# A chain of two transformer blocks on one core: the feed-forward network in seven block products, its weights' sums on VectorE, the modulation beside the dilated attention, block-diagonal states

## The chip, the core and the metric

The kernel runs on one core of a Trainium2 chip. The core has a matrix engine (TensorE, PE in the rows; its weight loads are listed apart as PEld), a vector engine (VectorE, DVE), a scalar engine (ScalarE, ACT), a general engine (GpSimd, POOL) and SyncE (SP), which here only issues DMAs. The metric is the device time of one execution in microseconds (us). Matrix results land in eight banks of PSUM of 128 x 512 fp32; everything else works in SBUF, 128 partitions wide.

## The reference

x has 512 tokens of 1024 features. The first block has two layers (i = 0 with a pooling mixer, i = 1 with dilated attention); the second has two layers with three branches. Cut to what matters here:

```python
def _swiglu(x, w_gate, w_up, w_down):          # 1024 -> 2816 -> 1024
    return (jax.nn.silu(x @ w_gate) * (x @ w_up)) @ w_down

def first_block(x, ...):
    for i in range(DEPTH):                     # DEPTH = 2
        h = _swiglu(x, ffn1_w_gate[i], ffn1_w_up[i], ffn1_w_down[i])
        x = _layer_norm(ALPHA * x + MACARON_WEIGHT * h, ln_gain[i, 0], ln_bias[i, 0])
        m = _pool_mixer(...) if i % N_MIXERS == 0 else _dilated_attention_mixer(...)
        x = _layer_norm(ALPHA * x + m, ln_gain[i, 1], ln_bias[i, 1])
        h = _swiglu(x, ffn2_w_gate[i], ffn2_w_up[i], ffn2_w_down[i])
        x = _layer_norm(ALPHA * x + MACARON_WEIGHT * h, ln_gain[i, 2], ln_bias[i, 2])

def second_block(x, c, ...):
    c_act = jax.nn.silu(c)
    for l in range(DEPTH):
        mod = c_act @ ada_w[l] + ada_b[l]      # the modulation: one row of 3 x 1024
        shift, scale, gate = jnp.split(mod, 3, axis=-1)
        h = rms_norm(x, pre_norm[l]) * (1.0 + scale[:, None]) + shift[:, None]
        p = split_proj(h @ w_in[l])
        # retention and gla: 4 heads, keys of 64, values of 128; per chunk
        #   o = scores @ v + q @ state;  state = decay * state + k.T @ v
        # dsa_attention: sparse attention over the top 128 keys; then the merge
        x = x + gate[:, None] * rms_norm(y, post_norm[l])
```

## The kernel before

**Arithmetic.** Large products are made from split operands: a = h + l, h the rounded copy in the matrix engine's fast fp32 format and l the rest. `mm3` makes three matmuls of them, h·h, h·l and l·h (in the trace L146 to L148). The class `Stream` feeds weights: it loads chunks of up to 1 MB through SP's queue into two raw buffers (`wraw`), cuts them into parts of 128 x 1024 and splits each: ScalarE makes `wh` (L75), VectorE `wl` = raw - wh (L76), every fifth part GpSimd. It runs four parts ahead of the products (`split_ahead`), with five buffers each.

**Stages.** In the profile: first network of layer 0 from 10 to 384 us, pooling mixer to 489, second network to 858; layer 1: first network to 1246, dilated attention to 1860, second network to 2217; then the second block's layers to 2788 and 3362.

**The network (`ffn`).** Its 2816 hidden columns are 22 tiles of 128, in two halves of 12 and 10. A pair of tiles, called a unit in what follows, takes four parts of weights (two of gate, two of up) and 4 x 24 matmuls of 512 columns (eight contraction rows, three each). ScalarE makes silu (L366) and the split's h (L373); VectorE the product (L370) and the split's l (L374). The first four parts are done in two halves of the tokens (`f1_first`, 192 matmuls of 256 columns), since the last tokens' input comes late: it goes through transpositions on PE (L259), ScalarE (`xTh`, L267) and VectorE (`xTl`, L268). After a half, `f2` makes the down product of its rows, 512 columns of the output at a time, and VectorE adds it to x (L384, L386). In the last down product the last 8 rows of weights are kept back and done token tile by token tile (`tail=8`), and the layer norm of a tile (`layer_norm_tile`, L275 to L292) follows as soon as it has its sum; the next stage's transpositions follow that.

**Modulation.** `ada` makes shift, scale and gate with VectorE (L923, 192 operations on weights that GpSimd's queue loads, L920), sums over partitions with a product of ones on PE (L940, L941) and sends the rows to memory. A background generator (`early`, rate 0.09) is advanced by the foreground's ticks and spreads this over the first four stages.

**States.** In `retention` and `gla` the four heads of a token tile are done in two halves (p), each on 64 partitions of the queries: per half two matmuls of 128 columns with the scores and, from the second tile on, two with the state (L1171 and L1173; L1363 and L1365), into one bank per half.

**Order.** Each engine works through its own instructions in order. The Tile framework's scheduler decides that order when the kernel is built, from the order of the code and the dependences; PSUM banks and SBUF buffers are handed on when their last reader is done. In the dilated attention the scores of a group go PE (L675), VectorE (bias, L690, and row maximum, L693), ScalarE (exponential, L694), PE (transposition, L701), ScalarE (L703), PE (values, L713 and L717).

## Time and profile before

| | |
|---|---|
| median of 3 runs | 3365.49 us (3364.72 to 3367.86) |
| profiled execution | 3364.3 us |
| its span, first to last instruction | 3362.2 us |
| granted TensorE clock, mean | 0.999 |
| busy: PE, PEld, DVE, ACT, POOL | 99%, 80%, 49%, 34%, 15% |
| DMA, mean | 98 GB/s |

Busy time of overlapping matmuls is counted once. A row's duration of a matmul of 512 columns is some 0.4 us, more than the distance to the next one's start, since matmuls are pipelined: what one costs is read from starts. fp32 products that aren't split show two records per matmul. All rows of a helper have one line, so a tile's name tells where it belongs.

### The profile page before, as it was taken

The numbers are of one execution on the slowest core, as the hardware profiler recorded it, in microseconds if no ns is written. First come the engines' busy times: TensorE is split into PE (matmuls) and PEld (weight loads), VectorE is DVE, ScalarE is ACT, GpSimd is POOL, SyncE is SP. The second block draws the span as 40 slices with busy tenths as digits, with TensorE's granted clock in tenths as the row PEclk, the third lists the DMA queues.
The fourth block names the chain that finished last, engine by engine and source line by source line (L and its number), as shares of the span: only waits on it lengthen the run. The fifth ranks groups of instructions, "written<-read, shape, count | busy, mean of one in ns | idle before, by whom it ended". The sixth has DMA issues, their size and how long they took to land.

```text
span 3362.2 us, 44608 instructions
## 1 busy us (share of the span) xinstructions
PE 3326.0 (99%) x18469; PEld 2685.8 (80%) x18469; DVE 1663.9 (49%) x2936; ACT 1151.5 (34%) x1769; POOL 502.7 (15%) x558
## 2 busy tenths in 40 slices
PE   9999999999999999999999999999999999999998
PEld 7888888888888888788787888878778788777877
DVE  4444773334643353433435432366864736594563
ACT  3222233222222224444444322233434533343442
POOL 2211211212211121111110100021111001111000
PEclk9999999999999999999999999999999999999999
DMA  5433423333433223222222323232122332222222
GB/s 169 137 116 125 146 95 108 117 121 129 132 122 110 94 69 107 64 71 69 82 70 76 119 88 100 94 104 89 57 82 75 108 100 92 69 82 76 76 88 75
DMA packets 278771, 328.29 MB, mean 98 GB/s; under 512 B 10197, under 2 KB 222393, under 8 KB 278569
## 3 DMA queue, kind: packets, MB, share of 16 engines
q1 hardware_dynamic: 268504, 294.36, 26.5%
q0 software_dynamic: 9920, 31.03, 2.9%
q8 instruction: 145, 2.38, 0.3%
q14 instruction: 58, 0.47, 0.0%
q10 hardware_dynamic: 144, 0.07, 0.0%
HBM read 319.10 MB, written 6.32 MB: 97 GB/s over the span
## 4 chain that ended last, share of the span: by engine, by line
PE 90%; DVE 6%; DMA 1%; issue 1%; POOL 1%; ACT 1%; POOLq 0%; DVEq 0%; ACTq 0%
PE bank L146 27%; PE bank L148 27%; PE bank L147 27%; PE bank L701 1%; DVE wl L76 1%; PE bank L675 1%; DVE work L1115 1%; DVE m L1114 1%; PE bank L713 1%; PE bank L1077 1%; PE bank L717 1%; DMA adaw<-in_ada_w_dram 1%; PE bank L1417 1%; PE bank L1399 1%; PE bank L259 0%
## 5 line engine op out<-in xcount | busy, mean ns | idle before, releaser
L75 ACT ACTIVATE wh<-wraw 128x1024 fp32r<-128x1024 f32 (+1 forms) x528 | 554.1, 1052 | 1351.9 <-PE bank L147 616.1
L146 PE MATMUL bank<-xTh,wh 128*128 128x512 f32 (+1 forms) x2624 | 1009.5, 385 | 3.0 <-ACT wh L75 1.8
L147 PE MATMUL bank<-xTl,wh 128*128 128x512 f32 (+1 forms) x2624 | 996.6, 380 | 2.5 <-DVE xTl L268 2.5
L148 PE MATMUL bank<-xTh,wl 128*128 128x512 f32 (+1 forms) x2624 | 996.7, 380 | 0.7 <-DVE wl L76 0.7
L76 DVE TENSOR_TENSOR wl<-wraw,wh 128x1024 fp32r<-128x1024 f32 (+1 forms) x422 | 521.7, 1237 | 730.2 <-ACT wh L75 724.8
L146 PEld LDWEIGHTS bank<-xTh,wh 128*128 128x128 f32 x2624 | 494.7, 189 | 118.8 <-issue 15.6
L148 PEld LDWEIGHTS bank<-xTh,wl 128*128 128x128 f32 x2624 | 495.5, 189 | 103.7 <-DVE wl L76 1.2
L147 PEld LDWEIGHTS bank<-xTl,wh 128*128 128x128 f32 x2624 | 496.1, 189 | 98.4 <-DVE xTl L268 3.0
L76 POOL TENSOR_TENSOR wl<-wraw,wh 128x1024 fp32r<-128x1024 f32 (+1 forms) x106 | 255.6, 2411 | 1595.2 <-ACT wh L75 1525.8
L146 PE MATMUL bank<-wh,xTh 128*128 128x512 f32 (+2 forms) x1024 | 372.1, 364 | 1.4 <-ACT xTh L267 1.4
L148 PE MATMUL bank<-wh,xTl 128*128 128x512 f32 (+2 forms) x1024 | 363.9, 356 | 0.6 <-DVE xTl L268 0.6
L147 PE MATMUL bank<-wl,xTh 128*128 128x512 f32 (+2 forms) x1024 | 363.6, 355 | 0.0
L146 PE MATMUL bank<-wh,ah 128*128 128x512 f32 x704 | 278.3, 395 | 0.0
L148 PE MATMUL bank<-wh,al 128*128 128x512 f32 x704 | 278.0, 395 | 0.0
L147 PE MATMUL bank<-wl,ah 128*128 128x512 f32 x704 | 278.0, 395 | 0.0
L146 PEld LDWEIGHTS bank<-wh,xTh 128*128 128x128 f32 x1024 | 192.5, 188 | 33.6 <-ACT xTh L267 2.4
L148 PEld LDWEIGHTS bank<-wh,xTl 128*128 128x128 f32 x1024 | 192.6, 188 | 30.0 <-DVE xTl L268 1.1
L147 PEld LDWEIGHTS bank<-wl,xTh 128*128 128x128 f32 x1024 | 193.0, 188 | 26.1 <-issue 0.4
L923 DVE SCALAR_TENSOR_TENSOR modn<-adaw,cols,modn 128x256 f32<-128x256 f32 x192 | 101.4, 532 | 185.7 <-DMA adaw<-in_ada_w_dram 182.1
L370 DVE SCALAR_TENSOR_TENSOR v<-g,bank 128x512 f32<-128x512 f32 x88 | 60.5, 688 | 259.2 <-PE bank L148 255.7
L148 PEld LDWEIGHTS bank<-wh,al 128*128 128x128 f32 x704 | 132.2, 188 | 31.9
L146 PEld LDWEIGHTS bank<-wh,ah 128*128 128x128 f32 x704 | 132.3, 188 | 31.6
(354 smaller groups left out, 3256.9 us busy)
## 6 DMA issues: line engine op xcount, KB each, us to landing
wraw<-in_w_in_dram SPq DMA_DIRECT2D x58, 1024.0 KB, 4.8
wraw<-in_ffn_w_gate_dram SPq DMA_DIRECT2D x43, 1024.0 KB, 4.9
wraw<-in_ffn_w_up_dram SPq DMA_DIRECT2D x43, 1024.0 KB, 4.9
wraw<-in_ffn_w_down_dram SPq DMA_DIRECT2D x40, 1024.0 KB, 5.0
wraw<-in_attn_w_qkv_dram SPq DMA_DIRECT2D x56, 512.0 KB, 3.6
adaw<-in_ada_w_dram POOLq DMA_DIRECT2D x96, 256.0 KB, 3.4
wraw<-in_attn_w_qkv_dram SPq DMA_DIRECT2D x8, 1024.0 KB, 5.4
wraw<-in_w_out_dram SPq DMA_DIRECT2D x8, 1024.0 KB, 5.0
```

The source lines that it names most:

```text
L75: nc.scalar.activation(h, raw, AF.Copy)
L76: (nc.gpsimd if self.nsplit % POOL_EVERY == 1 else nc.vector).tensor_tensor(lo, raw, f32(h), ALU.subtract)
L146: nc.tensor.matmul(ps, s[0], m[0], start=start, stop=False)
L147: nc.tensor.matmul(ps, s[0], m[1], start=False, stop=False)
L148: nc.tensor.matmul(ps, s[1], m[0], start=False, stop=stop)
L370: nc.vector.scalar_tensor_tensor(v, gs[j - 2], 0.5, ps, op0=ALU.mult, op1=ALU.mult)
L675: nc.tensor.matmul(ps[g - 1][r * 32:(r + 1) * 32, 256:], q[g][:, r * P + i * 32:r * P + (i + 1) * 32], kk[g][:, :, r * P:(r + 1) * P], sta ...
L701: nc.tensor.transpose(ps[:, j * P:(j + 1) * P], p[:, j * P:(j + 1) * P], k.ident)
L713: nc.tensor.matmul(ps[c:c + 64, :E], t[:, j * P + c:j * P + c + 64], v0[:, i + j, hh, :], start=j == 0, stop=False, tile_position=(0, c))
L717: nc.tensor.matmul(ps[r * 32:(r + 1) * 32, :E], t[:, (g + 1) * P + r * 32:(g + 1) * P + (r + 1) * 32], vr[g - 1][r][:, h, :], start=False, ...
L923: nc.vector.scalar_tensor_tensor(m, w[:, i, :], k.cols["c_2"][:, kt:kt + 1], m, op0=ALU.mult, op1=ALU.add)
L1077: k.nc.tensor.matmul(ps[:, :n], q, ks[i][:, g, :n], start=i == 0, stop=i == 1)
```

## The change

1. **Gate and up as seven products.** The hidden columns are 11 units of 256, in four groups (`FF_PARTS`). The first unit of a network is done as before. For each other one, tokens (two halves), contraction (two halves) and columns (gate, up) make 2 x 2 blocks, and seven products of blocks take the place of eight: 7 x 24 matmuls of 256 columns. Four sums of weight blocks per unit are made on VectorE, in place in the raw buffers but one (`wsum`), from a second pair of raw buffers (`wraw2`) for up; the sums of input blocks (`token_sums`) once per network. All parts of units are split by ScalarE and VectorE, none by GpSimd. Products share banks: what one bank holds after one product is read out (copy by ScalarE, L528ff.) and the next product is added on.
2. **The down product** comes in four groups, and `tail` is 4.
3. **Modulation** is a background generator at rate 0.38 beside the dilated attention, drained after it, with rows of 256 columns.
4. **States** are kept block-diagonal, 128 x 256 for a pair of heads with zeros (GpSimd) where keys and values belong to different heads; `gather_heads` makes four matmuls of 128 columns and two of 256 on all 128 partitions into one bank.

```diff
+class Units:
...
+    def order(self):
+        res = []
+        for u in range(len(self.units)):
+            res.append((u, "b11"))
+            if u:
+                res.append((u - 1, "t4"))
+            res.append((u, "b21"))
+            if u:
+                res.append((u - 1, "b22"))
+            res += [(u, n) for n in ("t2", "t1", "t3")]
+        return res + [(len(self.units) - 1, n) for n in ("b22", "t4")]
...
+    def block(self, own, what):
...
+        if what == "t2":
+            t3 = K.wsum.tile([P, n * b11.shape[2]], F32, name="wsum", tag="wsum").rearrange("p (a b) -> p a b", a=n)
+            self.sums[own] = t3
+            add(t3, b22, b12, ALU.subtract)
+            add(b11, t3, b11, ALU.add)
+        elif what == "t1":
+            add(b12, b22, b11, ALU.subtract)
+        elif what == "t4":
+            add(b21, b21, b11, ALU.subtract)
...
-            (nc.gpsimd if self.nsplit % POOL_EVERY == 1 else nc.vector).tensor_tensor(lo, raw, f32(h), ALU.subtract)
+            pool = self.nsplit % POOL_EVERY == 1 and not isinstance(what, str)
+            (nc.gpsimd if pool else nc.vector).tensor_tensor(lo, raw, f32(h), ALU.subtract)
...
-FF_HALVES = ((0, 12), (12, 22))
+FF_PARTS = ((0, 3), (3, 6), (6, 9), (9, 11))
+HS = S // 2
...
+def token_sums(k, pool, tmp):
...
+    for n in ("a11", "a21", "a22"):
+        whole(n)
+    a11, a21, a22 = [full[n] for n in ("a11", "a21", "a22")]
+    V.tensor_tensor(a22, a21, a22, ALU.add)
+    V.tensor_tensor(a21, a11, a21, ALU.subtract)
+    new("s1")
+    nc.scalar.activation(res["s1"][0], a22, AF.Copy)
+    V.tensor_tensor(a11, a22, a11, ALU.subtract)
+    V.tensor_tensor(res["s1"][1], a22, f32(res["s1"][0]), ALU.subtract)
...
-def ffn(k, st, a, name, i, lnj, post, tail=8):
+def ffn(k, st, a, name, i, lnj, post, tail=4):
...
+        def product(bank, name, first=False, last=False):
+            h, lo = st.next()
+            ah, al = A[name]
+            for j in range(2):
+                cs = slice(j * P, (j + 1) * P)
+                o = bank[:, j * HS:(j + 1) * HS]
+                for kt in range(4):
+                    for n, (x, y) in enumerate(((h, ah), (h, al), (lo, ah))):
+                        nc.tensor.matmul(o, x[:, kt, cs], y[:, kt, :], start=first and j == kt == n == 0,
+                                         stop=last and kt == 3 and n == 2, skip_group_check=True)
+                    k.tick(0.5)
+        def unit(u, before):
...
+            product(b, "a11", first=True)
+            p1 = tp2("ta")
+            nc.scalar.activation(p1, b, AF.Copy)
+            before(0)
+            ba = k.bank()
+            product(ba, "a12", first=True, last=True)
+            V.tensor_tensor(p1, p1, ba, ALU.add)
+            nc.scalar.activation(p1, p1, AF.Silu)
+            before(1)
+            product(b, "s2")
...
+            product(bc, "s1", first=True)
+            product(b, "s3")
...
+            V.tensor_tensor(c22, u3, bc, ALU.add)
+        def rest(u, s, step):
...
+                product(b, "a22", last=True)
...
+                V.scalar_tensor_tensor(c22, g2, 0.5, c22, op0=ALU.mult, op1=ALU.mult)
...
+                product(bc, "s4", last=True)
+                V.tensor_tensor(u2, u2, bc, ALU.add)
+                V.scalar_tensor_tensor(u2, g1, 0.5, u2, op0=ALU.mult, op1=ALU.mult)
...
+def gather_heads(k, at, v, q, state):
+    b = k.bank()
+    for h in range(RH):
+        k.nc.tensor.matmul(b[:, h * P:(h + 1) * P], at(h), v[:, h * P:(h + 1) * P], start=h == 0,
+                           stop=state is None and h == RH - 1, skip_group_check=True)
+    if state is not None:
         for hp in range(2):
+            k.nc.tensor.matmul(b[:, 2 * hp * P:(2 * hp + 2) * P], q(hp), state[:, hp, :, :].rearrange("p s e -> p (s e)"),
+                               start=False, stop=hp == 1, skip_group_check=True)
...
             if dilated:
                 k.drain()
+                k.bg(modulation(), 0.38, slow=True)
                 dilated_mixer(k, st, a, 1)
+                k.drain(slow=True)
```

**A unit on VectorE.** In the last network, before, VectorE's order has the low parts of weights (`wl`) between the gated products (`v`) and their splits (`al`):

```order
L370 SCALAR_TENSOR_TENSOR v_15289<-g_15225,bank_15260 128x512
L76 TENSOR_TENSOR wl_15334<-wraw_15228,wh_15333 128x1024
L374 TENSOR_TENSOR al_15292<-v_15289,ah_15291 128x512
L370 SCALAR_TENSOR_TENSOR v_15326<-g_15258,bank_15295 128x512
L76 TENSOR_TENSOR wl_15367<-wraw_15296,wh_15366 128x1024
L374 TENSOR_TENSOR al_15329<-v_15326,ah_15328 128x512
L76 TENSOR_TENSOR wl_15435<-wraw_15364,wh_15434 128x1024
L370 SCALAR_TENSOR_TENSOR v_15425<-g_15361,bank_15396 128x512
L76 TENSOR_TENSOR wl_15470<-wraw_15364,wh_15469 128x1024
L374 TENSOR_TENSOR al_15428<-v_15425,ah_15427 128x512
```

Now a unit there reads so; `wsum` and the `wraw` written are sums of weight blocks, `ta`, `tb` and `tc` results read out of banks:

```order
L145 TENSOR_TENSOR wl_19257<-wraw_19088,wh_19256 128x1024
L563 TENSOR_TENSOR tb_19056<-tb_19056,bank_19058 128x512
L145 TENSOR_TENSOR wl_19289<-wraw_18870,wh_19288 128x1024
L564 SCALAR_TENSOR_TENSOR tb_19056<-ta_18995,tb_19056 128x512
L120 TENSOR_TENSOR wraw_19088<-wsum_19382,wraw_19088 128x1024
L145 TENSOR_TENSOR wl_19319<-wraw_19088,wh_19318 128x1024
L494 TENSOR_TENSOR al_19153<-tb_19056,ah_19152 128x2x256
L122 TENSOR_TENSOR wraw_19154<-wraw_19154,wraw_19088 128x1024
L145 TENSOR_TENSOR wl_19351<-wraw_18872,wh_19350 128x1024
L124 TENSOR_TENSOR wraw_19088<-wraw_19088 128x1024
L145 TENSOR_TENSOR wl_19386<-wraw_19088,wh_19385 128x1024
L546 TENSOR_TENSOR tc_19346<-tc_19346,bank_19286 128x512
```

Three of the four sums of the next unit (L120, L122, L124) stand in VectorE's order among the low parts and gated products of the unit before; the fourth, L119, three rows ahead of these.

**The start of a network on VectorE.** In the second network, before, the last token tile's norm (`x3_80`) and the transposed input's low parts (`xTl`) were followed by two rows of the modulation and the weights:

```order
L268 TENSOR_TENSOR xTl_94<-bank_3845,xTh_93 128x4x128
L292 SCALAR_TENSOR_TENSOR x3_80<-x3_80,rstd_3734,B_2792 128x1024
L268 TENSOR_TENSOR xTl_94<-bank_3852,xTh_93 128x4x128
L268 TENSOR_TENSOR xTl_94<-bank_3859,xTh_93 128x4x128
L268 TENSOR_TENSOR xTl_94<-bank_3866,xTh_93 128x4x128
L943 COPY modn0_531<-bank_3888 128x512
L930 TENSOR_TENSOR adal_3926<-modn1_532,adah_3925 128x512
L76 TENSOR_TENSOR wl_4027<-wraw_3763,wh_4026 128x1024
L370 SCALAR_TENSOR_TENSOR v_4007<-g_4003,bank_3771 128x512
L76 TENSOR_TENSOR wl_4031<-wraw_3763,wh_4030 128x1024
```

Now sums of the input (`a11` to `a22`, `s1l`) and of weights stand there:

```order
L440 TENSOR_TENSOR a11_4741<-xTh_93,xTl_94 128x1024
L347 TENSOR_TENSOR xTl_94<-bank_4607,xTh_93 128x4x128
L347 TENSOR_TENSOR xTl_94<-bank_4614,xTh_93 128x4x128
L440 TENSOR_TENSOR a21_4743<-xTh_93,xTl_94 128x1024
L440 TENSOR_TENSOR a22_4745<-xTh_93,xTl_94 128x1024
L119 TENSOR_TENSOR wsum_4784<-wraw_4499 128x1024
L453 TENSOR_TENSOR a22_4745<-a21_4743,a22_4745 128x1024
L120 TENSOR_TENSOR wraw_4497<-wsum_4784,wraw_4497 128x1024
L454 TENSOR_TENSOR a21_4743<-a11_4741,a21_4743 128x1024
L458 TENSOR_TENSOR s1l_4750<-a22_4745,s1h_4749 128x1024
L457 TENSOR_TENSOR a11_4741<-a22_4745,a11_4741 128x1024
L145 TENSOR_TENSOR wl_4781<-wraw_4497,wh_4780 128x1024
```

Nine further rows follow (four of 512 columns and five of 1024) up to the low part of the first unit's t2 (`wl_4788`).

**The dilated attention on VectorE.** Before, bias (`sc`) and row maximum (`m`) of the scores stood with rows of the attention alone:

```order
L690 SCALAR_TENSOR_TENSOR sc<-dist,bank 128x256
L690 SCALAR_TENSOR_TENSOR sc<-dist,bank 128x128 x2
L690 SCALAR_TENSOR_TENSOR sc<-dist,bank 128x256
L693 TENSOR_REDUCE m<-sc 128x1
L690 SCALAR_TENSOR_TENSOR sc<-dist,bank 128x128 x2
L693 TENSOR_REDUCE m<-sc 128x1
L595 TENSOR_TENSOR q_12926<-bank,q_12926 64x4x4x32
```

Now the modulation's rows (`adam`, on the loaded `adaw`) stand among them:

```order
L896 SCALAR_TENSOR_TENSOR sc<-dist,bank 128x128 x2
L896 SCALAR_TENSOR_TENSOR sc<-dist,bank 128x256
L899 TENSOR_REDUCE m<-sc 128x1
L896 SCALAR_TENSOR_TENSOR sc<-dist,bank 128x128 x2
L1132 SCALAR_TENSOR_TENSOR adam<-adaw,cols,adam 128x256
L899 TENSOR_REDUCE m<-sc 128x1
L1132 SCALAR_TENSOR_TENSOR adam<-adaw,cols,adam 128x256 x2
L928 RECIPROCAL rc<-bank 128x1
L1132 SCALAR_TENSOR_TENSOR adam<-adaw,cols,adam 128x256
L931 TENSOR_SCALAR on<-bank,rc 128x64
L1132 SCALAR_TENSOR_TENSOR adam<-adaw,cols,adam 128x256
L145 TENSOR_TENSOR wl<-wraw,wh 128x1024
```

A row of `adam` whose weights are not there yet holds the rows below it.

## Rows read from the trace of the kernel before

**Rows 1.** The page: busy us (share of span) x instructions; the ending chain.

```profile
PE 3326.0 (99%) x18469; PEld 2685.8 (80%) x18469; DVE 1663.9 (49%) x2936; ACT 1151.5 (34%) x1769; POOL 502.7 (15%) x558
...
PE 90%; DVE 6%; DMA 1%; issue 1%; POOL 1%; ACT 1%; POOLq 0%; DVEq 0%; ACTq 0%
```

**Rows 2.** PE's waits: line, releaser: us in all, times, longest us.

```profile
PE bank L1283 <- DVE gz L1265: 7.1, 3, 3.9
...
PE bank L147 <- DVE xTl L268: 2.5, 2, 1.3
PE bank L259 <- DVE z L964: 2.1, 1, 2.1
```

**Rows 3.** Groups by line and shape: count | busy us, mean ns | idle before.

```profile
L75 ACT ACTIVATE wh<-wraw 128x1024 fp32r<-128x1024 f32 x516 | 545.6, 1059 | 1345.0 <-PE bank L147 615.2 <-PE bank L148 366.5 <-issue 281.2
L76 DVE TENSOR_TENSOR wl<-wraw,wh 128x1024 fp32r<-128x1024 f32 x413 | 514.3, 1246 | 725.3 <-ACT wh L75 720.0 <-PE bank L940 3.6
...
L76 POOL TENSOR_TENSOR wl<-wraw,wh 128x1024 fp32r<-128x1024 f32 x103 | 250.2, 2430 | 1557.6 <-ACT wh L75 1488.1 <-PE bank L1046 28.1 <-issue 26.1
...
L366 ACT ACTIVATE g<-bank 128x512 f32<-128x512 f32 x88 | 51.0, 579 | 0.0
```

**Rows 4.** PE's timeline from 539.60, first and last of 152: start, duration.

```profile
539.60 0.40 PE L148 MATMUL bank<-xTh,wl 128*128 128x512 f32 x1
...
574.97 0.40 PE L147 MATMUL bank<-xTl,wh 128*128 128x512 f32 x1
```

**Rows 5.** PE's timeline of 256 columns, 68 rows; engines' busy time within.

```profile
497.70 0.28 PE L148 MATMUL bank<-xTh,wl 128*128 128x256 f32 x1
...
505.56 0.28 PE L148 MATMUL bank<-xTh,wl 128*128 128x256 f32 x1
...
498.00:505.00 7.00, 7.00 (x62) 7.00 (x62) 6.74 (x10) 1.34 (x2) 1.45 (x1) 1.00 0.67 212
```

**Rows 6.** PE's timeline in retention, a half tile's products and four alike.

```profile
2336.55 0.60 PE L1171 MATMUL bank<-rv,rat 128*128 128x128 f32 x4
...
2346.70 0.38 PE L1171 MATMUL bank<-rv,rat 128*128 128x128 f32 x2
2347.01 0.49 PE L1173 MATMUL bank<-kv,rqk 64*128 64x128 f32 x2
...
2347.84 0.49 PE L1173 MATMUL bank<-kv,rqk 64*128 64x128 f32 x2
2348.26 0.51 PE L146 MATMUL bank<-xTh,wh 128*128 128x512 f32 x1
```

**Rows 7.** DVE's timeline in a network: start us, duration us.

```profile
334.19 1.22 DVE L76 TENSOR_TENSOR wl<-wraw,wh 128x1024 fp32r<-128x1024 f32 x1
335.32 0.48 DVE L923 SCALAR_TENSOR_TENSOR modn<-adaw,cols,modn 128x256 f32<-128x256 f32 x1
335.72 0.68 DVE L374 TENSOR_TENSOR al<-v,ah 128x512 fp32r<-128x512 f32 x1
```

**Rows 8.** DVE's and PE's timelines, second network, last transposed input.

```profile
506.94 1.29 DVE L268 TENSOR_TENSOR xTl<-bank,xTh 128x512 fp32r<-128x512 f32 x2 [2.11 <-ACT xTh L267]
...
506.47 0.36 PE L146 MATMUL bank<-xTh,wh 128*128 128x256 f32 x1
```

**Rows 9.** DVE's timeline at a network's end, one token tile to the next.

```profile
377.05 0.67 DVE L386 TENSOR_TENSOR x<-x,bank 128x512 f32<-128x512 f32 x1
...
381.85 0.69 DVE L386 TENSOR_TENSOR x<-x,bank 128x512 f32<-128x512 f32 x1
```

**Rows 10.** Dilated attention: PE PEld DVE ACT POOL busy; DVE's wait for modulation weights.

```profile
1246.00:1860.00 614.00, 612.09 (x4968) 488.53 (x4967) 265.66 (x554) 268.87 (x399) 94.09 (x134) 1.00 0.25 76
...
DVE modn L923 <- DMA adaw<-in_ada_w_dram: 182.1, 66, 5.7
```

**Rows 11.** ACT's and PE's timelines in dilated attention: exponential, then transposition.

```profile
1615.54 0.68 ACT L694 ACTIVATE sc<-sc,m 128x512 f32<-128x512 f32 x1
...
1617.35 0.33 PE L701 MATMUL bank<-ident,sc 128*128 128x128 f32 x1
```

More of the change, by code (lines that the diff above doesn't have):

```diff
@@ L30, with __init__ @@
 POOL_EVERY = 5
+class Units:
+    def __init__(self, units):
+        self.units = units
+    def order(self):
[9 more added lines that the diff above has]
+        return res + [(len(self.units) - 1, n) for n in ("b22", "t4")]
 class Stream:
-    def __init__(self, K, chunks, ahead):
+    def __init__(self, K, plan, ahead):
         self.K = K
-        self.chunks = chunks
-        self.parts = [(ci, p) for ci, (_, ps) in enumerate(chunks) for p in ps]
+        self.chunks = []
+        self.parts = []
+        for c in plan:
+            n = len(self.chunks)
+            if isinstance(c, Units):
+                for first, second in c.units:
+                    self.chunks += [(first, 0), (second, 1)]
+                for u, what in c.order():
+                    own = (n + 2 * u, n + 2 * u + 1)
+                    self.parts.append((own, what, {"t4": own[:1], "b22": own[1:]}.get(what, ())))
+                continue
+            src, ps = c
+            self.chunks.append((src, 0))
+            self.parts += [((n,), p, (n,) if i == len(ps) - 1 else ()) for i, p in enumerate(ps)]
+        self.place = []
+        count = [0, 0]
+        for _, q in self.chunks:
+            self.place.append(count[q])
+            count[q] += 1
+        self.gone = [set(), set()]
+        self.left = [0, 0]
         self.raw = {}
+        self.sums = {}
         self.ready = {}
@@ L61, in load @@
             self.nload += 1
+    def block(self, own, what):
+        K = self.K
+        first, second = [self.raw.get(c) for c in own]
+        n = (second if first is None else first).shape[1] // 2
+        b11, b21 = (None, None) if first is None else (first[:, :n], first[:, n:])
+        b12, b22 = (None, None) if second is None else (second[:, :n], second[:, n:])
+        add = K.nc.vector.tensor_tensor
+        if what == "t2":
[7 more added lines that the diff above has]
+            add(b21, b21, b11, ALU.subtract)
+        return {"b11": b11, "b21": b21, "b22": b22, "t1": b12, "t2": b11, "t4": b21, "t3": self.sums.get(own)}[what]
     def split(self, upto):
@@ L388, in evac @@
                         k.pend.append(layer_norm_tile(k, tp, t, G, B, post))
-                f2(k, st, acts.get, list(range(f0, f1)), 512, evac, tail=tail if fin else 0)
+                act = lambda kt: [x[:, kt % 2, :] for x in acts[kt // 2]]
+                f2(k, st, act, list(range(2 * u0, 2 * u1)), 512, evac, tail=tail if fin and c == 1 else 0)
         k.recent = None
@@ L1161, in scores @@
[L1161 to L1173 removed]
+            for p in range(2):
+                rows = slice(p * 64, p * 64 + 64)
+                nc.tensor.matmul(ps[p][:, hp * P:(hp + 1) * P], qk[rows, 2 + hp, ts], qk[rows, hp, ts], start=True, stop=True)
```

350 lines of the change are left out of this document (203 added, 147 removed).

## The prediction

> **What bounds the kernel now.** I read the page's busy times first and its chain of waits second. TensorE (PE) is busy 99% of the span and the chain runs through it for 90%; VectorE (DVE) is busy 49% [rows 1]. Third comes the list of what PE waits for: its largest entries are 7.1, 2.5 and 2.1 us [rows 2]. So PE's issue rate is the whole time, and a change counts only by the time that PE needs and by the waits it creates on PE. As rows of matmuls overlap, I take their cost from start to start. In the first feed-forward network after the pool mixer 152 matmuls of 512 columns start from 539.60 to 574.97: 35.37/151 = 0.2342 us each [rows 4]. There 68 of 256 columns start from 497.70 to 505.56: 7.86/67 = 0.1173 us each [rows 5]. Half the columns cost half the time, although weights are loaded without a pause there (PEld busy 7.00 of 7.00 us, same rows).
>
> By the Trainium skill's page TensorE: Matmul & The Clock Gate, section "Back-to-back issue gap", the spacing in a stream of load and matmul is set by both operations, and N/2.4 + 2.5 ns under-counts small matmuls (81 ns for 56 at N = 128); with those 25 ns on top of its 109 at N = 256, my estimate is 134 ns, and the change would save nothing in its units. The trace disagrees at 256 columns, with 117 ns against 234.
>
> The profiled execution took 3364.3 us, 2.1 more than its span; the median is 3365.5. I sum against 3364.3 and add 1.2 at the end.
>
> **The change part by part.**
>
> *Block products.* Each of the four networks has eleven units; ten become seven products of 24 matmuls of 256 columns. A unit was 96 x 0.2342 = 22.48 us and becomes 168 x 0.1173 = 19.71. 40 x 2.78 = 111 us less, if PE never waits.
>
> *VectorE in a unit.* Now eleven operations of 1024 columns (seven low parts, four sums) and seven of 512, where it had three or four low parts and four of 512. An operation of 1024 takes 1.22 us alone and 1.13 when another follows; of 512, 0.68 and 0.60 (starts 334.19, 335.32, 335.72) [rows 7]. So 16.6 to 18.4 us of PE's 19.7: 84 to 93%. GpSimd (POOL) no longer takes a part in five, which cost it 2430 ns [rows 3]. The splits run up to four parts, 11 us, ahead of PE, and with this lead VectorE has 1.3 us per unit to spare. I take 0 in the steady state; if the lead is lost, see case D. Where a group of units ends (16 places), the last two products stand alone: the last waits for ScalarE's copy (0.58, row of L366 [rows 3]) and an addition (0.69), 1.8 us with the hand-overs, under eleven matmuls of the product before and the four to seven of the down product that the order puts between, 2.2 to 2.9 us. From 0 to 0.5 each; 4 us, at most 8.
>
> *Start of a network.* The block products need sums of the transposed input. After the last low part of it, which begins at 506.94 and ends at 508.2 [rows 8], 14 operations of 1024 (1.2 us with hand-overs) and four of 512 (0.65) stand in VectorE's order up to the low part of t2: 19.4 us, to 527.6. PE has 120 matmuls of unit 0 left from 506.47 (14.1 us, to 520.5) and two products (5.6 us), and wants it at 526.1. It waits 1.5 us, and as much again for t1, 4.3 us later on VectorE and 2.8 on PE: 3 us. Four networks: +13 (0 to 25, as nothing else there gets longer).
>
> *End of a network.* The last down product was done token by token over 8 rows of weights, 24 matmuls or 5.62 us per tile, and now over 4: 2.81. VectorE's work on a tile, addition and layer norm, takes 4.80 us (377.05 to the same row at 381.85) [rows 9]. Before, it hid; PE waited 2.1 us at the worst end [rows 2]. Now PE passes from the tail to the next stage with 48 x 0.2342 = 11.2 us, 72 matmuls of 256 (8.4) and three transpositions of 0.8 (505.68, after the last row of [rows 5], to 506.47 [rows 8]): 22.0 us. VectorE ends the fourth tile at 2.8 + 4 x 4.80 = 22.0, plus some 5 us of transposed low parts (four of 512) and weight parts (two of 1024) between: 27.3. 5 us each, 6 at the last, whose transformation adds two operations: +21.5 (10 to 30).
>
> *Block-diagonal states.* A token tile with a state took two halves, and one half (two matmuls of 128 columns and two on 64 rows, each two records) goes from 2346.70 to 2348.26 and lets the next matmul start 0.1 late: 1.66 us [rows 6], 3.3 per tile. Now four matmuls of 128 columns are eight records of (0.60 - 0.38)/2 = 0.11 us (four records at 2336.55 and two at 2346.70 in the same rows), 0.88, and two of 256 columns four records of twice that, 0.88: with 0.1, 1.86. That is 1.46 less for 12 tiles (three tiles, retention and gated attention, two layers): -18. At the least nothing, if the one bank is waited for; I take the rows. The scores' new order is worth 0 to -5; I take -2. GpSimd's zero halves lie beside PE.
>
> *Down product and loads.* It comes in four parts instead of two, so 16 more additions of 512 columns per network (0.68 [rows 7]) beside its matmuls, where VectorE has only low parts to make: 0. The weights loaded are the same bytes.
>
> *Modulation.* PE does the same products. In the networks the old place cost nothing that a row shows. Beside the dilated attention VectorE is busy 265.66 of 614 us [rows 10], so there is room for 176 operations of 0.48 us (row at 335.32 [rows 7]; 16 of the 192 go early), 84 us. But VectorE works in order, and its queue there holds the attention's scores. Before, it waited 66 times for these weights, 182.1 us, 2.76 each [rows 10]; with two of four loads not ahead, 44 such waits remain. Behind each stand reduction, exponential and PE's transposition. The tight chain has little room: the exponential at 1615.54 lasts 0.68, and PE transposes it at 1617.35 [rows 11], 1.1 us later. A wait of 2.76 in it would cost 1.7; a sixth of the 44 in it is 12 us. The ends are 0 (all beside the chain) and 44 x 2.76 = 121 (all on it); the 614 us have many rows that are not in the chain, so I stay near 0: +12.
>
> **Sum.** -111 - 18 - 2 + 4 + 13 + 21.5 + 12 = -80.5; 3364.3 - 80.5 + 1.2 = 3285 us.
>
> **The rivals.**
>
> B: the stalls hide. VectorE's start and end queues may run back to back at 1.13 and 0.60, and the modulation fall between chains: 3285 less 0.75 x 50 = 3248. For it: before, no wait for a layer norm's output or a transposed low part is above 2.5 us [rows 2]. Against: 27.3 against 22.0 us is no close call.
>
> C: the dilated stage pays three times as much (36 instead of 12) and units lose 0.25 us each (10): 3285 + 34 = 3319. For it: 2.76 us per wait against a room of 1.1.
>
> D, slower than before: VectorE becomes the bound in the units. It is in order, and each of the four sums needs ScalarE's copy (L75, 1.06 us [rows 3]) before its low part can follow; if nothing lies between, that is 18.4 + 4 x 1.16 = 23.0 us per unit against PE's 19.7, 3.3 x 40 = 132: 3417. It costs from 19.7 on, and undoes the whole gain from 19.7 + 80/40 = 21.7. Against it: in the new order other rows stand between a sum and its low part.
>
> E, slower too: the dilated stage waits for every one of the 44 loads: 3285 - 12 + 121 = 3394; it eats the gain from 92/44 = 2.1 us per wait.
>
> F: matmuls of 256 columns don't keep 0.1173 us in long streams (from 0.2342 x 96/168 = 0.134 the units give nothing): 3285 + 111 = 3396. Only 68 of them stand in [rows 5], at an even pace. It is what the Trainium skill's section named above would make of the change.
>
> **How the numbers follow.** A 0.48, B 0.17, C 0.18, D 0.13 (0.05 of it only in part, near no change), E 0.03, F 0.01. About 0.2%, 7 us, is what a measurement of this kernel can tell from no change. Faster: A, B and C, 0.83; same: D in part, 0.05; slower: 0.12. The range runs from 3238 (B, and 10 us more where its stalls fall to their lower ends) to 3344 (C with the starts at their upper bound, 25 for 13, and the ends at 30 for 21.5, less a few), leaving out D, E, F and a little of B and C.
>
> **What would show it.** The mean start-to-start time of L146 to L148's counterparts in a unit should be 0.117 us, and the unit 19.7. The list of PE's waits should have low parts of weights and of sums at each network's start (3 us) and the layer norm's output before transpositions at its end (5 us each). VectorE should be busy 85 to 93% in units; if PE's waits for weights' low parts recur in every unit, D is right. In the dilated stage the span should be 614 + 12 us, with VectorE waiting for the modulation's weights some 44 times. The states' products should take 1.9 us a tile. I am wrong if stalls on PE add up to over 110 us, or under 15.

## The result, and the profile after

The changed kernel takes 3271.85 us (median of 4 runs, 3270.23 to 3275.69) for 3365.72 of the kernel before beside it: a ratio of 0.9722, 95% interval 0.9705 to 0.9739, or 94 us less. The forecast was 3285.

The page's first part and its chain, after, as [rows 1]:

```profile
PE 3202.8 (98%) x21325; PEld 2750.6 (84%) x21325; DVE 2175.3 (67%) x3517; ACT 1360.8 (42%) x2025; POOL 442.1 (14%) x529
...
PE 71%; DVE 11%; issue 2%; DMA 2%; POOL 1%; ACT 1%; POOLq 0%; DVEq 0%; ACTq 0%
```

PE is still the bound (98%), with 123 us less of busy time, while VectorE rose from 49 to 67%. The chain still runs mostly through PE, but by 71% for 90%: it now crosses to VectorE more often.

By stages the gain is not spread evenly. A stage is taken here from the start of the last token tile's transposition at its entry to the same point of the next stage, to within a microsecond. The rows are those of the window view (length, then PE, PEld, VectorE, ScalarE and GpSimd busy; granted clock, DMA share, GB/s), after: the four networks, with the dilated stage as the fourth row, and the second block's layers.

```profile
24.78:379.79 355.01, 349.39 (x2441) 324.74 (x2440) 270.52 (x325) 151.46 (x189) 26.32 (x20) 1.00 0.33 107
485.48:837.40 351.92, 347.96 (x2434) 323.82 (x2433) 258.08 (x281) 148.31 (x182) 19.39 (x9) 1.00 0.30 101
837.40:1187.82 350.42, 347.87 (x2435) 324.37 (x2436) 256.53 (x284) 148.33 (x182) 20.23 (x21) 1.00 0.32 104
1187.82:1817.44 629.62, 615.41 (x4982) 491.46 (x4983) 362.00 (x766) 272.97 (x417) 190.76 (x293) 0.99 0.36 109
1817.44:2173.05 355.61, 349.01 (x2392) 323.93 (x2391) 257.42 (x287) 152.93 (x194) 25.62 (x20) 0.99 0.31 103
...
2173.05:2725.21 552.16, 544.45 (x3037) 436.10 (x3036) 352.80 (x737) 227.45 (x414) 71.74 (x80) 1.00 0.27 90
2725.21:3269.70 544.49, 528.93 (x2963) 423.10 (x2961) 330.24 (x698) 213.45 (x384) 67.23 (x69) 1.00 0.24 80
```

| stage | before | after | difference |
|---|---|---|---|
| networks 1 to 4 | 375.4, 378.8, 379.2, 377.9 | 355.0, 351.9, 350.4, 355.6 | -98.3 |
| pooling mixer, start | 106.7, 23.6 | 105.7, 24.8 | +0.2 |
| dilated stage | 607.2 | 629.6 | +22.4 |
| second block, two layers | 557.9, 555.5 | 552.2, 544.5 | -16.8 |

PE's waits after, in all, times and longest (before: [rows 2]):

```profile
PE bank L1141 <- ACT adah L1136: 9.0, 2, 8.2
...
PE bank L520 <- DVE wl L145: 5.4, 4, 2.8
...
PE bank L338 <- DVE z L1166: 5.1, 1, 5.1
PE bank L338 <- DVE x L371: 4.3, 5, 1.4
```

The first is the modulation's own product, the second the networks' starts, the last two the networks' ends.

**A unit.** PE's timeline in the second network (start, duration), to hold beside [rows 4, 5]: the first matmul of a unit's product with s1, then the first and last of the products on the input's tiles; the last row is the window view up to the next unit's first matmul with s1.

```profile
602.90 0.28 PE L520 MATMUL bank<-s1h,wh 128*128 128x256 f32 x1
...
605.78 0.28 PE L520 MATMUL bank<-xTh,wh 128*128 128x256 f32 x1
...
616.92 0.28 PE L520 MATMUL bank<-xTh,wl 128*128 128x256 f32 x1
...
602.90:622.80 19.90, 19.90 (x171) 19.90 (x170) 16.96 (x19) 11.05 (x14) 0.00 (x0) 1.00 0.37 114
```

The unit takes 19.90 us. The 96 matmuls on the input's tiles (three blocks of the input, and the sum s3, which `token_sums` writes over the fourth) go at (616.92 - 605.78)/95 = 0.1173 us, as forecast; the 72 on the sums s1, s2 and s4, which have tiles of their own, at 0.1200 (s1: 2.76 us for 23 steps). VectorE is busy 16.96 us of the unit, the last row says, near the lower end of the forecast's 16.6 to 18.4, and GpSimd not at all.

**The down product** got faster, which no step foresaw. After, 137 matmuls in a row:

```profile
178.74 0.39 PE L226 MATMUL bank<-wl,ah 128*128 128x512 f32 x1
...
209.56 0.39 PE L227 MATMUL bank<-wh,al 128*128 128x512 f32 x1
```

That is 30.82/136 = 0.2266 us each; before, 288 in a row from 151.6 to 218.6 went at 0.2333. For all 2112 of them it would be 14 us. But 44 of a network's 528, at the edges of parts and of token tiles, don't reach this pace: added up from start to start, without PE's waits and the half clock at the last network's end, the down products of the four networks took 492.8 us before and 483.9 after, 9 us less.

**States**, after, as [rows 6], a whole tile with state:

```profile
2281.58 1.05 PE L1356 MATMUL bank<-rv,rat 128*128 128x128 f32 x8
2282.47 1.03 PE L1360 MATMUL bank<-kv,rqk 128*128 128x256 f32 x4
2283.15 0.58 PE L225 MATMUL bank<-xTh,wh 128*128 128x512 f32 x1
```

1.57 us, and the next matmul 0.2 late: 1.8, where the forecast had 1.86.

**The dilated stage's largest wait.** VectorE, the issue of a load by GpSimd, PE, and the window view behind the wait (its last three numbers: granted clock, DMA share, GB/s):

```profile
1210.90 4.03 DVE L1132 SCALAR_TENSOR_TENSOR adam<-adaw,cols,adam 128x256 f32<-128x256 f32 x4
1218.81 1.00 DVE L1132 SCALAR_TENSOR_TENSOR adam<-adaw,cols,adam 128x256 f32<-128x256 f32 x2 [3.88 <-DMA adaw<-in_ada_w_dram]
...
1214.19 0.77 POOL L1129 DMA_DIRECT2D adaw<-in_ada_w_dram  x1 [0.58 <-DVE adam L1132]
...
1220.36 0.58 PE L1141 MATMUL bank<-adah,ones_r 128*128 128x256 f32 x1 [8.15 <-ACT adah L1136]
1220.74 0.63 PE L225 MATMUL bank<-xTh,wh 128*128 128x512 f32 x1
1221.17 0.63 PE L226 MATMUL bank<-xTl,wh 128*128 128x512 f32 x1
...
1220.36:1224.00 3.64, 3.64 (x10) 2.96 (x11) 1.33 (x3) 1.02 (x2) 1.30 (x3) 0.50 0.28 79
```

Two rows of the modulation on VectorE wait 3.88 us for a load; ScalarE's copy and PE's product of ones need their sum, and PE, which has this product next in its order, stands for 8.15 us. So the load is not all of it: before it VectorE spent 4.03 us on four earlier rows of the same sum, where a row mostly takes 0.48, while GpSimd split a part of weights (1210.99 to 1213.60); one of the two buffers came free only in the course of these, and GpSimd issued the next load at 1214.19. The matmuls behind the wait start 0.43 us apart, and 0.23 to 0.24 apart some 4 us later: the granted clock was 0.50 in the first 3.64 us, the lower of its two levels.

### The profile page after: what moved, and what is told of

Read it like the earlier page. It is cut to its first block, busy times and chain, and to the rows that moved or that the text cites. A ratio compares the mean times of both kernels' runs of the same rounds, so it can differ in the third digit from the quotient of the medians.

```text
span 3269.7 us, 51439 instructions
## 1 busy us (share of the span) xinstructions
PE 3202.8 (98%) x21325; PEld 2750.6 (84%) x21325; DVE 2175.3 (67%) x3517; ACT 1360.8 (42%) x2025; POOL 442.1 (14%) x529
## 3 DMA queue, kind: packets, MB, share of 16 engines
q1 hardware_dynamic: 268632, 294.36, 27.3%
## 4 chain that ended last, share of the span: by engine, by line
PE 71%; DVE 11%; issue 2%; DMA 2%; POOL 1%; ACT 1%; POOLq 0%; DVEq 0%; ACTq 0%
PE bank L225 16%; PE bank L520 16%; PE bank L227 16%; PE bank L226 16%; DVE wl L145 2%; PE bank L907 1%; DVE work L1317 1%; PE bank L881 1%; DVE m L1316 1%; PE bank L1279 1%; PE bank L919 1%; PE bank L1623 1%; PE bank L923 1%; PE bank L1605 1%; DMA adaw<-in_ada_w_dram 1%
## 5 line engine op out<-in xcount | busy, mean ns | idle before, releaser
L143 ACT ACTIVATE wh<-wraw 128x1024 fp32r<-128x1024 f32 (+1 forms) x608 | 638.2, 1053 | 953.6 <-PE bank L227 287.5
L145 DVE TENSOR_TENSOR wl<-wraw,wh 128x1024 fp32r<-128x1024 f32 (+1 forms) x535 | 660.2, 1236 | 531.0 <-ACT wh L143 528.2
L225 PE MATMUL bank<-xTh,wh 128*128 128x512 f32 (+1 forms) x1344 | 502.5, 375 | 3.4 <-ACT wh L143 2.2
L227 PE MATMUL bank<-xTh,wl 128*128 128x512 f32 (+1 forms) x1344 | 490.5, 365 | 2.0 <-POOL wl L145 1.0
L226 PE MATMUL bank<-xTl,wh 128*128 128x512 f32 (+1 forms) x1344 | 489.7, 365 | 2.6 <-DVE xTl L347 1.3
L145 POOL TENSOR_TENSOR wl<-wraw,wh 128x1024 fp32r<-128x1024 f32 (+1 forms) x73 | 177.8, 2436 | 1963.6 <-ACT wh L143 1682.8
L520 PE MATMUL bank<-xTh,wh 128*128 128x256 f32 x1280 | 360.3, 281 | 1.3 <-ACT tc L544 1.1
L520 PE MATMUL bank<-xTl,wh 128*128 128x256 f32 x1280 | 358.3, 280 | 0.0
L520 PE MATMUL bank<-xTh,wl 128*128 128x256 f32 x1280 | 358.3, 280 | 0.0
L225 PEld LDWEIGHTS bank<-wh,xTh 128*128 128x128 f32 x1024 | 192.5, 188 | 31.8 <-ACT xTh L346 2.4
```

The costliest lines, as they stand in the source:

```text
L143: nc.scalar.activation(h, raw, AF.Copy)
L145: (nc.gpsimd if pool else nc.vector).tensor_tensor(lo, raw, f32(h), ALU.subtract)
L225: nc.tensor.matmul(ps, s[0], m[0], start=start, stop=False)
L226: nc.tensor.matmul(ps, s[0], m[1], start=False, stop=False)
L227: nc.tensor.matmul(ps, s[1], m[0], start=False, stop=stop)
L520: nc.tensor.matmul(o, x[:, kt, cs], y[:, kt, :], start=first and j == kt == n == 0, stop=last and kt == 3 and n == 2, skip_group_check=True)
```

## The experiments

Each is an edit of the changed kernel (3271.85; ratio 0.9722).

**1. The states of before.** `key_values`, `retention` and the end of `gla` as they were:

```diff
-        po = gather_heads(k, lambda h: W[n][:, h * P:(h + 1) * P], v[:, n, :],
-                          lambda hp: qe[:, hp, n * P:(n + 1) * P], st[n])
+        for p, b in enumerate(po):
+            rows = slice(p * 64, p * 64 + 64)
+            for hp in range(2):
+                nc.tensor.matmul(o, W[n][:, cs], v[:, n, cs], start=True, stop=n == 0)
...
```

> The changed kernel with the states of before: two halves, two matmuls of 128 columns and two on 64 rows each. My theory (PE's issue time is the whole time): 3.3 us per tile with a state come back for 1.9, 12 tiles, and the scores' order: 16 to 20 us slower than the changed kernel's 3272, so 3288 to 3292, all of it in the second block's two layers. Rival (the second block is bound by waits of VectorE and ScalarE there, and the measured gain of 17 us in its layers comes from the new order): no more than 5 us, 3272 to 3277.

Measured: 3292.3 us, ratio 0.9781 (0.9767 to 0.9794), 20 us slower than the changed kernel. The second block's layers, in the window view:

```profile
2171.97:2736.27 564.30, 557.76 (x3062) 443.58 (x3060) 348.87 (x730) 227.72 (x420) 67.76 (x68) 0.99 0.27 88
2736.27:3289.80 553.53, 540.49 (x2987) 429.33 (x2985) 327.42 (x692) 213.08 (x390) 64.00 (x57) 1.00 0.24 79
```

They are 12.1 and 9.0 us longer than in the changed kernel. The theory holds: the new products are worth what their issue time says.

**2. The modulation in the networks again.**

```diff
             rope_tables(k, a)
             yield
+            yield from modulation()
...
-                k.bg(modulation(), 0.38, slow=True)
```

> The changed kernel with the modulation spread over the networks and the pooling mixer again (rate 0.09), in its new form of 256 columns. In the changed kernel the dilated stage became 22 us longer: 5.6 us of the products moved there, 13 us of PE's waits (8.2 of them in one for the modulation's own product) and about 3 us at half clock behind them. Theory: the old place would cost little in networks, as VectorE's order there has room of about 1 us per unit and the modulation adds 84 us of VectorE over three networks and a mixer, 2 us per unit of 30: VectorE passes PE's 20 us per unit in the units that carry it, +0 to 30 us there; -17 in the dilated stage: 3255 to 3285, the dilated stage back at 607 us. Rival (VectorE in units is already the bound, every operation counts): 84 us more there, 3272 - 17 + 84 = 3339.

Measured: 3381.28 us, ratio 1.0047 (1.0034 to 1.006): 0.5% slower than the kernel before. Windows: networks 1 and 2, network 3 up to the first transposition behind it (334.0 us in the changed kernel), from there to the last one (16.5), the dilated stage:

```profile
24.30:410.93 386.63, 360.28 (x2444) 333.10 (x2443) 287.29 (x359) 152.75 (x193) 58.00 (x78) 0.97 0.33 110
524.06:899.74 375.68, 355.49 (x2448) 329.25 (x2447) 280.60 (x345) 150.44 (x189) 58.87 (x80) 0.98 0.34 112
899.74:1252.73 352.99, 338.10 (x2337) 314.83 (x2337) 264.86 (x318) 144.76 (x180) 52.54 (x76) 0.99 0.36 116
1252.73:1319.30 66.57, 21.36 (x117) 18.62 (x118) 30.53 (x58) 6.16 (x11) 28.30 (x54) 0.62 0.26 75
1319.30:1926.55 607.25, 605.67 (x4938) 483.35 (x4937) 259.87 (x545) 265.14 (x395) 82.38 (x109) 1.00 0.25 76
```

The dilated stage is back at 607, as the theory said, but the networks and the mixer cost 82 us more than in the changed kernel, as the rival said, and four blocks of the modulation's columns, left over, are drained before the dilated stage, in 66.6 us with PE busy 21, which neither side had expected. The theory falls for the networks. But VectorE is busy only 75% there, which isn't a bound by load; experiments 5, 6 and 8 separate load from waits.

**3. The modulation's product issued later.**

```diff
-        yield
-        yield
+        for _ in range(6):
+            yield
         ps = k.bank()
...
-                k.bg(modulation(), 0.38, slow=True)
+                k.bg(modulation(), 0.60, slow=True)
```

> The changed kernel, with the modulation's product of ones six steps behind its low part (two before) and the background rate 0.60 (0.38). Theory: PE's wait of 8.2 us for the modulation's own product, and the half clock behind it, go: 8 to 11 us faster, 3261 to 3264. Rival: what PE waited for was VectorE's queue held by loads of modulation weights, so the wait moves to the attention's own operations behind the same rows: within 3 us of 3272, or slower, as the steps now come faster.

Measured: 3271.28 us, ratio 0.9719 (0.9705 to 0.9732): nothing. The longest wait is still there:

```profile
PE bank L1141 <- ACT adah L1136: 8.9, 2, 8.0
```

The time is the rival's, its reason isn't: the wait moved nowhere. In PE's order the first four products, the fourth of which is the one that waits, stand at the same places in both kernels: the steps in the code didn't set the scheduler's order here. So this run doesn't tell what a later product would bring.

**4. A tail of six.**

```diff
-FF_PARTS = ((0, 3), (3, 6), (6, 9), (9, 11))
+FF_PARTS = ((0, 2), (2, 5), (5, 8), (8, 11))
...
-def ffn(k, st, a, name, i, lnj, post, tail=4):
+def ffn(k, st, a, name, i, lnj, post, tail=6):
```

> The changed kernel with the last group of units of three (groups 2, 3, 3, 3) and the last down product token by token over 6 rows of weights, 18 matmuls per tile (4.2 us) for 12 (2.8). Theory: PE's waits for the layer norm's output at the networks' ends, some 13 us in all with the half clock at the last, fall to those of before (about 4): 5 to 9 us faster, 3263 to 3267. Rival: the waits at the ends come from the order of the last transpositions and not from the tail, and stay: within 3 us of 3272.

Measured: 3263.91 us, ratio 0.9695 (0.9682 to 0.9708). The size is the theory's, the reason isn't. The fourth network and the dilated stage:

```profile
1188.50:1809.52 621.02, 613.65 (x4985) 490.37 (x4983) 361.37 (x762) 272.63 (x417) 190.56 (x287) 1.00 0.37 111
1809.52:2165.95 356.43, 348.27 (x2392) 323.39 (x2391) 263.55 (x291) 154.39 (x197) 25.59 (x18) 0.99 0.31 101
...
1177.88 0.39 PE L226 MATMUL bank<-xTl,wh 128*128 128x256 f32 x1 [2.10 <-DVE xTl L347]
PE bank L338 <- DVE z L1166: 5.8, 1, 5.8
```

The networks together are as long as before the edit (the fourth 356.4 for 355.6): where the wait for a norm's output went, one for the transposed low part came (2.10 us), and the last wait is 5.8. The 8.6 us came in the dilated stage (621.0 for 629.6), whose order the edit had shifted: the wait for the modulation's product is 1.6 us there, and the longest of all 1.7.

**5 and 6. More load on VectorE in a unit.** Sums made twice, and three times:

```diff
             add(t3, b22, b12, ALU.subtract)
+            add(t3, b22, b12, ALU.subtract)
...
             add(b12, b22, b11, ALU.subtract)
+            add(b12, b22, b11, ALU.subtract)
```

> The changed kernel with two of the four weight sums of each unit (t3 and t1) made twice: two more operations of 128x1024 on VectorE per unit, 80 in all, 96 us of VectorE's time, none that waits for another engine. Theory (VectorE has room in units: 16.6 to 18.4 us of some 20): 18.9 to 20.8 us per unit, just at PE's pace: 0 to 15 us slower, 3272 to 3287. Rival (VectorE's order is already the bound in units, as the 82 us that the modulation cost in the networks suggest): some 96 us slower, 3350 to 3370.

> The same with both sums made three times: four more operations of 128x1024 per unit, 192 us of VectorE's time. Theory: 21.1 to 23.2 us of VectorE per unit against 20.0 of PE: VectorE is the bound, 1.1 to 3.2 us per unit and what it does to the clock: 45 to 130 us slower, 3317 to 3400. Rival (VectorE was the bound all along): 190 us slower, 3460.

Measured: 3295.88 us, ratio 0.9781 (0.9765 to 0.9798), and 3320.25 us, ratio 0.9858 (0.9843 to 0.9872): 24 and 48 us for 96 and 192 us of work. A unit in the second network with four more:

```profile
604.98:624.88 19.90, 19.90 (x170) 19.90 (x169) 18.73 (x20) 10.63 (x13) 0.00 (x0) 1.00 0.35 107
...
PE bank L524 <- ACT wh L147: 21.1, 10, 4.4
```

VectorE is busy 18.73 us and the unit still takes 19.90 us (so does the median of 24 units in each of the three kernels). With four more the four networks are 49 us longer; 31 of these lie between a network's start and its first product with s1, where PE waits for parts (the second row), the others in the first units and at the edges of groups. Two more cost more than the theory's 15 us. The rival is out, and so is the theory's bound at 21 us. From one down product to the next, in the changed kernel and with four more:

```profile
574.20:636.00 61.80, 61.80 (x513) 61.16 (x512) 46.88 (x48) 31.62 (x39) 2.42 (x1) 1.00 0.37 120
...
596.20:659.50 63.30, 62.13 (x513) 61.22 (x512) 57.73 (x58) 31.67 (x39) 2.91 (x1) 1.00 0.36 117
```

VectorE's share rises from 76 to 91% and stays below the bound. It works ahead during the down product, where it has less to do: in the one behind this stretch of the changed kernel (636.0 to 666.8) it makes three of the next unit's four sums (L120, L122, L124).

**7. The sums' layout.**

```diff
-    new("s1")
+    pair = [pool.tile([P, 4, S], F32R, name="s12" + x) for x in "hl"]
+    res["s1"] = [x[:, :, :HS] for x in pair]
+    res["s2"] = [x[:, :, HS:] for x in pair]
```

> The changed kernel, with the input's sums s1 and s2 (high parts in one tile, low parts in another) side by side, so that a block's 256 columns have the stride of 512 that the blocks of the input itself have; s4 stays as it was, its rows next to each other. In the changed kernel products with blocks of the input go at 0.1173 us per matmul, those with s1, s2 and s4 at 0.1200. Theory: the layout of the moving operand sets this; s1 and s2 fall to 0.1173 and s4 stays: 40 units x 48 x 0.0027 = 5 us faster, 3267. Rival: it is the place in SBUF, or the sum's own writers, and the pace of s1 and s2 stays at 0.1200: within 1 us of 3272, pace unchanged.

Measured: 3272.8 us, ratio 0.9719 (0.9704 to 0.9733). The first and last of 48 matmuls on the pair:

```profile
599.53 0.28 PE L521 MATMUL bank<-s12h,wh 128*128 128x256 f32 x1
...
605.17 0.28 PE L521 MATMUL bank<-s12h,wl 128*128 128x256 f32 x1
```

5.64/47 = 0.1200 us: the pace stays, as the rival said. The stride doesn't set it, and the sum's writers don't either: s3 is a sum too, split by the same lines, but it lies in the input's tiles, and its matmuls are among the 96 at 0.1173 us. What is left is the tile itself, its place or its size; this was not tried.

**8. No loads for the modulation**, in the networks (on experiment 2) and beside the dilated attention:

```diff
-            w = alloc("adaw", F32)
-            k.pin(w)
...
+            if j == q == 0:
+                w = alloc("adaw", F32)
+                k.pin(w)
...
```

> The kernel with the modulation in the networks (e2), but its weights are loaded once per layer, 256 KB, and every operation reads these: all 192 VectorE operations and all products stay, 94 of 96 loads are left out (the modulation's values are not the reference's). In e2 the networks and the mixer took 82 us more than in the changed kernel for 84 us of VectorE, and draining the rest before the dilated stage 50 us. Theory (VectorE works in order, and rows of the network wait behind rows whose weights are not there yet): the 82 fall to a quarter of VectorE's time, as in e6a and e6b, plus the products, 25 to 30 us, and the drain to some 25: 3381 - 55 - 25 = 3300. Rival (VectorE's time itself, and rows that fall badly, cost the 82): only the drain gets shorter, 3355.

> The changed kernel with the modulation beside the dilated attention, and the same loads left out. Theory: the 12 us of PE's waits there and the half clock behind them are waits for loads, passed on by VectorE's order; what stays are the products (5.6) and VectorE's time: the stage goes from 630 to 613 to 618 us, the kernel from 3272 to 3256 to 3260. Rival (rows between scores and their maximum cost by their own time): no more than 4 us of gain.

Measured: 3302.21 us, ratio 0.9803 (0.9788 to 0.9817), and 3262.12 us, ratio 0.9685 (0.9669 to 0.9701). In the networks (the stretches of experiment 2) and in the dilated stage:

```profile
23.32:382.20 358.88, 351.09 (x2445) 325.73 (x2443) 292.20 (x370) 152.78 (x193) 27.81 (x31) 1.00 0.30 101
489.52:846.40 356.88, 350.40 (x2449) 325.72 (x2447) 284.13 (x341) 150.63 (x189) 30.88 (x34) 1.00 0.31 100
846.40:1192.21 345.81, 338.72 (x2336) 316.30 (x2337) 273.55 (x327) 145.58 (x181) 23.64 (x30) 0.99 0.31 100
1192.21:1235.00 42.79, 18.61 (x119) 16.60 (x118) 25.47 (x49) 5.79 (x10) 20.86 (x41) 0.68 0.16 50
...
1187.15:1803.70 616.55, 612.06 (x4983) 488.82 (x4983) 363.13 (x766) 272.99 (x417) 129.12 (x208) 1.00 0.25 75
```

The same rows with their weights already there cost the networks and the mixer 22 us instead of 82, and the dilated stage is 616.5 us long for 629.6. The theory holds in both (the second kernel is 2 us above its range): what the modulation costs is mostly its loads, which VectorE's order hands on to rows of the network or of the attention. The edit leaves out the loads' traffic too, but that did not slow the network's own loads: ScalarE waits for these (gate, up and down weights) 31.8 us in experiment 2 and 38.8 here. The Trainium skill, on the page Perfetto Trace Analysis, section "Tensor Engine Instruction (MATMUL, LD_WEIGHTS)", calls the queues of ScalarE, VectorE and GpSimd strictly first in, first out; the 60 us less in the networks and the mixer agree.

**9. A lower rate.**

```diff
-                k.bg(modulation(), 0.38, slow=True)
+                k.bg(modulation(), 0.34, slow=True)
```

> The changed kernel with the modulation's background rate at 0.34 instead of 0.38, so that its 24 rows are spread over more of the dilated stage (it still ends before the stage does). Theory: PE's 12 us of waits in that stage come from loads of modulation weights that follow each other too fast for two buffers; with a tenth more time between them the wait of 8.2 us shrinks by some 3 us and the half clock behind it with it: 3 to 6 us faster, 3266 to 3269. Rival: the wait depends on the third row's place right at the start of the stage alone, and goes entirely or not at all: 0 or 10 us.

Measured: 3258.11 us, ratio 0.9675 (0.966 to 0.9689): 14 us faster than the changed kernel, more than either side said. The dilated stage:

```profile
1186.98:1805.38 618.40, 611.47 (x4982) 488.84 (x4983) 359.98 (x766) 270.96 (x417) 193.31 (x293) 1.00 0.37 111
```

It is 618.4 us long, 11.2 less; the wait of 8.15 is gone, and PE's list has none left for the modulation's product. That it goes whole is as the rival had it. VectorE's waits for the modulation's weights did not shrink (50.6 us in 31 waits in the changed kernel):

```profile
DVE adam L1132 <- DMA adaw<-in_ada_w_dram: 54.3, 31, 5.2
```

So the lower rate did not make VectorE wait less, as the theory had it; it moved the rows. The fourth product, the one that PE waited for, now stands some 27 matmuls later in PE's order, and what it needs is there by then.

**10. The lower rate with the tail of six, 0.34 and 0.32.**

```diff
-                k.bg(modulation(), 0.38, slow=True)
+                k.bg(modulation(), 0.34, slow=True)
...
+def ffn(k, st, a, name, i, lnj, post, tail=6):
```

> The changed kernel with both edits that helped: last group of three units with a tail of 6 rows, and the modulation's rate at 0.34. Theory (the two take away different waits, at the networks' ends and in the dilated stage): the gains add, 3272 - 8 - 13 = 3251, ratio to the kernel before 0.965. Rival (with the tail of 6 the modulation's long wait was gone already, 1.6 us for 8.2, so both edits took the same one): 3256 to 3264.

> The same with the rate at 0.32, the last of the modulation's 24 rows nearer to the stage's end. Theory: the rows stand further apart still, waits of the scores behind loads become fewer: 0 to 3 us below the kernel with 0.34. Rival: the wait left in the stage is set by where single rows fall among the scores, not by the rate: within 3 us on either side.

Measured: 3262.83 us, ratio 0.9691 (0.9678 to 0.9704), and 3258.94 us, ratio 0.9679 (0.9666 to 0.9692); the dilated stage takes 622.4 and 616.7 us. The gains don't add, as the first rival said: both edits had taken the same wait. The lower rate gained 3.9 us, a little more than either side said. Of all versions the one of experiment 9 is the fastest beside the last of these, 3258 and 3259 us.

## Why the prediction was right

The forecast, 3285 us, lay 13 us above the time, and the direction and the main term hold: PE's issue time is the whole time, and seven products at the pace of [rows 5] take the place of eight. That the sum came so near is in part luck: errors of +8, +5 and +3 us stand against -9, -8, -13 and -3. By its steps:

| term | forecast | measured | from |
|---|---|---|---|
| units | -111 | -103 | 40 x (22.48 - 19.90) |
| down product | 0 | -9 | 492.8 to 483.9 us, start to start |
| starts of networks | +13 | +5 | waits 2.8, 0.9, 0.9, 0.9 |
| ends of groups | +4 | +1 | waits 0.3, 0.5 |
| ends of networks | +21.5 | +8 | waits of 10.7 for 4.9, half clock 2 |
| states and scores | -20 | -17 | layers; experiment 1: 20 |
| modulation | +12 | +17 | +22.4 in its stage, less 5.6 of products that left the networks |

The measured column sums to -98; the stages give -92.5. Some 5 us are left unresolved; the first term takes all 40 units at 19.90, which only the 24 intervals inside groups show (20 of them to the hundredth). The working itself has three slips that carry nothing: four starts of 3 us are 12 and not 13; eleven operations of 1.22 us and seven of 0.68 are 18.2 and not 18.4; C with the starts and ends at their upper bounds is 3340 and not 3344.

*Units:* right in kind. The pace on the input's tiles was exact; that on s1, s2 and s4 is 0.0027 us slower, 0.2 us per unit. The rule that would have taken the gain away (the spacing of small matmuls) is refuted here by 168 matmuls in 19.90 us. That VectorE's steady state costs nothing was right, and experiments 5 and 6 show how far: four more operations per unit leave the unit at 19.90. Case D did not come: VectorE was busy 16.96 us of the unit, ScalarE's copies did not stand in its way, and part of the sums is made during the down product, which a unit taken alone leaves out.

*Starts:* mis-sized. Three of four waited 0.9 us for 3. The walk along VectorE's queue put 1.2 us on each operation, but the queue ran without a gap, and 1.13 is the row's own number for that [rows 7]. 14 x 0.07 and 4 x 0.05 are 1.2 us, and of the 1.5 us for t2's low part at most 0.1 is left. What PE waited for is the low part of the next product's block, t1: 0.9 us for 1.5. The first network waited 2.8 there, and 1.2 in the first kernel of experiment 8; why it differs was not tried.

*Ends:* mis-sized. VectorE's last rows of a norm, first network, after:

```profile
365.72 1.28 DVE L371 SCALAR_TENSOR_TENSOR x<-x,rstd,B 128x1024 f32<-128x1024 f32 x1
371.23 1.28 DVE L371 SCALAR_TENSOR_TENSOR x<-x,rstd,B 128x1024 f32<-128x1024 f32 x1
377.74 1.28 DVE L371 SCALAR_TENSOR_TENSOR x<-x,rstd,B 128x1024 f32<-128x1024 f32 x1 [0.44 <-POOL rstd L356]
...
379.08 0.33 PE L338 MATMUL bank<-ident,x 128*128 128x128 f32 x1 [0.22 <-DVE x L371]
```

The tiles follow each other by 5.5 and 6.5 us with the transposed parts and weights among them; the sum had 4.8 each and 5 us more on top, though the 4.8 of [rows 9] already held a half of the next tile's statistics. The last tile is through at 379.0, 24.7 us after the tail's start (27.3 in the sum), and PE waits 0.2 us for it, 1.9 us in all with the tiles before. At the last network the wait is 5.1 us, near the 6. Experiment 4 shows that a longer tail does not win this back: other waits come in its place.

*Modulation:* right in kind and direction, 5 us short. The sum had a sixth of 44 waits on the attention's chain. The rows show one wait of 8.15 us for the modulation's own product, which the step had not looked at, a wait of 2.04 for an exponential, smaller ones, and the half clock behind them. VectorE's own waits for the modulation's loads after:

```profile
DVE adam L1132 <- DMA adaw<-in_ada_w_dram: 50.6, 31, 3.9
...
DVE adam L1132 <- DMA adam<-in_ada_b_dram: 22.6, 12, 4.1
```

That is 31 waits for weights of 1.6 us, where the step had 44 of 2.76, and 12 for the bias row, which it did not count. That loads, handed on by VectorE's order, are the cause is shown by experiment 8; that the place of single rows decides, and not the sum of the waits, is what 4, 9 and 10 show: the stage varies from 617 to 630 us with the same work.

*States:* right, by experiment 1.

*What was missed:* the down product's pace, whose cause is open.

## What to carry to other kernels

Where one engine issues without a pause, count its instructions at their start-to-start time and the gain follows to within a tenth; walk a queue that runs without a gap at that time too, and not with stand-alone durations, which made the stalls at the starts too long here. An engine that is late in one stretch can catch up in the next, so look beyond one unit. Work in the background is priced by the waits that reach the main engine and not by its busy time: the same rows, some 80 us of VectorE, cost 82 us in the networks with loads and 22 without, while before, with more room on VectorE, 182 us of such waits showed in no row of PE [rows 2, 10]. A product that has to wait for background work stands in the main engine's order, so look for it there, and try a few rates before moving anything else.

## What the runs showed of the hardware

Matmuls of one shape ran at paces that differ with their operands' tiles: 0.1173 or 0.1200 us for 256 columns, and 0.2342, 0.2333 or 0.2267 for 512. For the 256 columns experiment 7 excludes the stride of the moving operand as the cause, and the product with s3 excludes that it is a sum; the tiles' places in SBUF weren't varied on their own. By the Trainium skill's page TensorE: Matmul & The Clock Gate, section "Back-to-back issue gap", the formula, given for an isolated matmul, gives 109 and 216 ns; every pace here is above it, by 5 to 10%. A pause of PE costs more than itself: after the 8.15 us the next matmuls took nearly twice their time at a granted clock of 0.50, and in the drain of experiment 2 the mean granted clock was 0.62.
